# Keys of the dilated heads: the low part in both halves of a tile per head, and score matmuls of 128 rows

## The chip, the cores and the metric

The kernel runs on one core of a Trainium2 chip. The metric is the device time of one execution in microseconds (us), as the median of several runs.

## What is computed

Two layers of a decoder trunk on 512 tokens of width 1024, all in float32. Each layer is a hybrid token mixer, a cross attention into 256 memory tokens and a squared-ReLU MLP, with norms around each. The mixer has eight latent heads and eight dilated heads of 64 features; the change concerns the dilated ones alone:

```python
z = h @ w_in
q_d, k_d, v_d = z[..., o3:o4], z[..., o4:o5], z[..., o5:]
...
s = jnp.einsum('brcqhd,brckhd->brchqk', qq, kk, preferred_element_type=jnp.float32) * scale + bias
s = jnp.where(mask, s, -jnp.inf)
...
e = jnp.exp(s - s_max)
```

The three dilation patterns are merged by their softmax denominators. The kernel therefore computes one dense causal score matrix per head and adds a table by distance, which holds the bias and the logarithm of the number of patterns that reach a pair.

## The kernel before

**Split numbers.** Every float32 operand of a large matmul is kept as a high part and a low part (its remainder) of type fp32r, and a product is summed from several matmuls: in the linear layers (`mm`, lines 193 to 200) high by low, low by high and high by high. The names in the profile are `whi`, `wlo` for weights, `xth`, `xtl` for inputs.

**Dilated queries and keys.** `feat_major` (lines 618 and 619) leaves two heads in one tile of 128 features by 512 tokens in PSUM, head `a` on partitions 64`a` to 64`a`+63. `ev_qd` (line 571) makes one tile `qs` per head: its high part on the head's own 64 partitions and its low part on the other 64. `ev_kd` (line 582) makes one tile `kh` per head with the high part in both halves: ScalarE (ACT) writes the head's own half (line 588), GpSimd (POOL) copies it to the other (line 590). The low parts of two heads, written by VectorE (DVE, line 591), lie in one shared tile `kl`.

**Scores.** `dilated_parts` (line 594) gives the two matmuls of a score tile. The first has 128 rows (contraction over all partitions): (high q, low q) by (high k, high k). The second has 64 rows: high q by low k. `scores` (line 411) walks over four query tiles i of 128 queries; each has these two matmuls (line 419) of N = 128(i+1) columns into a PSUM tile `sp` (two buffers), then DVE adds the table and takes the minimum (line 423), ACT takes the exponential (line 425), DVE the reciprocal of the sum (line 426), and POOL scales the rows (line 427). TensorE (PE) then transposes the rows (`ptp`, lines 431 to 449) and multiplies by the values (`op`, line 456). The eight latent heads use the same function with three matmuls of 96 rows each (`latent_parts`, operands named `ring`).

**What sets the order.** `attention` (line 776) runs the scores one head ahead of the transposes, and `weave` (line 217) puts steps of other linear layers (`ptm`, `pfm`) between its steps by an estimate of PE's work. The tile scheduler then fixes each engine's order. Weights arrive on SyncE's (SP) one DMA queue as `raw`, in turn with the table `tb` of each dilated head (line 624). Most tiles, `qs`, `kh`, `kl` and `tb` among them, come from one pool of 49 buffers of 128x512 (`unit`, line 63).

Of the kernel before, what the change touches and what calls it, by code (L numbers as in the profile page):

```python
# [34 lines left out]
SPLIT = True  # L35
SCORE_STEPS = (0, 1, 2)  # query tiles after which the scores let other work in
FINE = 2  # weight pieces in one step of a linear layer
MEM_AT = 30  # step of the latent layers at which the memory is read
STOP = object()
DELAY = 7.5  # tensor engine work (us) put between a norm and its transposes  # L40
RATIOS = (1.8, 1.1)  # other work by attention work: dilated heads, latent heads


@with_exitstack
def block_kernel(ctx: ExitStack, tc, x, mem, positions, rel_bias, w_in, q_norm_g, w_uq, kv_norm_g,
# [3 lines left out]
    nc = tc.nc  # L49
# [24 lines left out]

# [1 line left out]
    ident = const.tile([128, 128], F32, name="ident")  # L76
# [11 lines left out]
    def load_x(t, src=None):  # L88
        """The residual stays on chip but for the mixer's attention, over which it is kept in memory."""
        for n in range(2):  # L90
            xs[t][n] = unit("xs")
            rows, cols = slice(t * 128, (t + 1) * 128), slice(n * 512, (n + 1) * 512)
            nc.sync.dma_start(xs[t][n], x[0, rows, cols] if src is None else src[rows, cols])
# [10 lines left out]
    def gains(c0, parts):  # L104
        """Gains as columns c0.. of gT, features on partitions."""
        grow = unit("grow", (80, 128))
        n = 0
        for g in parts:
            rows = g.shape[0] * g.shape[1] // 128
            nc.sync.dma_start(grow[n:n + rows, :], g.rearrange("l (n p) -> (l n) p", p=128))  # L110
            n += rows
        gps = t_ps("gps")
        nc.tensor.transpose(gps[:, 0:n], grow[0:n, :], ident[0:n, 0:n])
        nc.vector.tensor_copy(gT[:, c0:c0 + n], gps[:, 0:n])
# [4 lines left out]

# [1 line left out]
    def rpow(m, name):  # L121
# [4 lines left out]
    def rstd_from(ss, width, name):  # L126
        """(ss / width + eps) ** -0.5"""
        m = small(name + "m", ss.shape[1])
        nc.vector.tensor_scalar(m, ss, 1.0 / width, EPS, op0=OP.mult, op1=OP.add)
        return rpow(m, name)  # L130

    def load_w(src, r0, kts, c0, width, gcol=None, heads=0):
        """Rows r0.. (kts tiles of 128), columns c0..c0+width, as parts for the tensor engine;
        heads: columns [head, 2, 64] are reordered to [2, head, 64]."""
        raw = wp.tile([128, 2, 512], F32, tag="raw", name="raw", bufs=3)
# [31 lines left out]

    # Order of emission: `clk` adds up the tensor engine's work so far; work that waits for a chain
    # on the other engines is put off until that much of it has been emitted.
    clk = [0.0]  # L170
# [46 lines left out]
    def weave(main, fills, ratio):  # L217
        """Emit main, and after each of its steps about ratio() times its work from fills, the first
        that is not held up; a step that is held up yields True."""
        owed = 0.0  # L220
# [22 lines left out]
    def with_at(gen, other, at):  # L243
        """gen, with a step of other after each of its steps from step `at` on."""
        i = 0
        for held in gen:
            yield held
            i += not held
            if i > at and not held:
                next(other, None)  # L250
        run(other)

    def tok_major_steps(src, c0, width, nk, gcol, xh, xl, tiles, evac, r0=0, whole=False, rot=0, early=()):
        """out[token, column] = sum_k X[k, token] W[k, column]; evac(t, psum).
        whole: one token tile after the other, all weights of the group resident."""
        ps = [None] * tiles
# [34 lines left out]
    def feat_major_steps(src, c0, ntile, nk, gcol, xh, xl, ntok, evac, whole=0):  # L291
        """out[column, token]; ntile column tiles of 128; evac(m, psum).
        whole: in that many parts of the tokens, all weights of the group resident."""
        ps = [None] * ntile
# [43 lines left out]
    def transposed(xn, n, dests, t):  # L338
        """Half n of a token tile, transposed into columns t of dests."""
        tp = t_ps("tp")  # L340
# [30 lines left out]
    def add_post_norm(ys, ms, t):  # L371
        """xs[t] += y * g * rstd(y); ys = y * g in two halves, ms = their parts of the mean square."""
        m = small("pnm", 1)
# [12 lines left out]
    def out_proj_steps(w, OTh, OTl, gb, after, rot=0):  # L386
        """token-major projection of the eight feature tiles, then post-norm into the residual."""
        ys = [[None, None] for _ in range(NT)]
# [22 lines left out]
    def scores(P, parts, tb, scale):  # L411
        """Causal softmax of one head: rows of queries, tile i at OFFS[i]."""
        nm = small("nm", 4)
# [17 lines left out]
    def transposed_scores(P, pts):  # L431
        """The softmax with keys on partitions: key tile j holds queries from tile j on."""
        PT = pp.tile([128, 1280], F32, tag="PT", name="PT", bufs=2)
# [17 lines left out]
    def weighted_values(PTs, v_of):  # L451
        """Two heads' outputs, features on partitions, as one feature tile."""
        op = mm_ps("op")
# [12 lines left out]
    def rotary_tables():  # L466
        # angles reduced by multiples of two pi in exact steps
        posi = unit("posi", (4, 128), I32)
# [29 lines left out]
    def distance_tables():  # L498
        # relative-position table by distance: bias + log(number of patterns that reach the pair)
        rb = const.tile([32, HEADS], F32, name="rb")  # L500
# [11 lines left out]

# [1 line left out]
    for l in range(DEPTH):  # L514
        # mixer input
        if l == 0:
# [25 lines left out]
        def rope(dst, src, t, n):  # L542
            """dst[:, n, 32] = rotated src[:, n, 32] (may be the same)."""
            cosb = cs[:, t, 0:1, :].to_broadcast([128, n, ROPE])
# [26 lines left out]
        def ev_qd(m, ps):  # L571
            """Head a at partitions 64a: its high part there, its low part in the other half."""
            for a in range(2):
# [8 lines left out]
        def ev_kd(m, ps):  # L582
            """The high part of each head in both halves; the low parts of the two heads in one tile."""
            lo = unit("kl", dt=WD) if SPLIT else None
            for a in range(2):
                here, there = slice(a * 64, a * 64 + 64), slice(64 - a * 64, 128 - a * 64)
                u = unit("kh", dt=WD)
                nc.scalar.activation(u[here, :], ps[here, :], AF.Copy)
                if SPLIT:
                    nc.gpsimd.tensor_scalar(u[there, :], u[here, :].bitcast(F32), 1.0, 1.0, op0=OP.mult, op1=OP.mult)  # L590
                    nc.vector.tensor_sub(lo[here, :], ps[here, :], u[here, :].bitcast(F32))
                kd.append((u, lo))

        def dilated_parts(h):
            here = slice(h % 2 * 64, h % 2 * 64 + 64)
            if not SPLIT:
                return [(qd[h][here, :], kd[h][0][here, :])]
            return [(qd[h], kd[h][0]), (qd[h][here, :], kd[h][1][here, :])]

# [32 lines left out]
        def latent():  # L632
            """Queries, keys (features on partitions) and values of the latent attention."""
            yield from tok_major_steps(wl, QL, KVL + ROPE, NK, gm, xh_t, xl_t, NT, ev_ckv, whole=True)
# [86 lines left out]
        def slot(h):  # L721
            """Parts of a head's queries and keys, in turn over four places."""
            r, c = ring[h % 4 // 2], h % 2 * 4
            return (r[:, c, :], r[:, c + 1, :]), (r[:, c + 2, :], r[:, c + 3, :])
# [20 lines left out]
        def memory():  # L745
            """Keys (features on partitions) and values of the memory."""
            mt = [(unit("mth", (128, 2, MEM), WD), unit("mtl", (128, 2, MEM), WD) if SPLIT else None)
# [28 lines left out]
        def attention():  # L776
            """Dilated heads, then latent heads; the scores run one head ahead."""
            P, PTs = [None] * 16, [None] * 16
# [33 lines left out]

        # cross attention
        qx = []
# [42 lines left out]
        def cross_transposed(h, P):  # L857
            """Keys on partitions, in parts: [key tile][part]."""
            PT = []
# [70 lines left out]

        # MLP
        gb = row_bcast(post_mlp_g, l)
# [48 lines left out]
def _shape_constants():  # L981
    """Index tables of the shapes: entry j stands for the distance 511 - j between query and key."""
    d = 511 - np.arange(640)
# [26 lines left out]
```

## Time and profile before

| | |
|---|---|
| median of 3 runs | 1589.37 us (1587.48 to 1592.85) |
| profiled execution, span from first to last instruction | 1589.2 us |
| PE busy / weight loads (PEld) | 1559.9 us (98%) / 1299.1 us (82%) |
| DVE / ACT / POOL busy | 820.2 (52%) / 706.8 (44%) / 229.5 us (14%) |
| mean granted TensorE clock | 0.995 of full speed |

The page gives busy time of each engine, the chain of work that ended last, and the costliest groups. The profile shows no other time of the profiled execution than its span. A matmul's recorded time is longer than its share of a stream, because matmuls overlap: what one costs is read from the distance between the starts of consecutive ones in the timeline. In its rows "128*128" stands for active rows by active columns of the array, and "128x384" for what streams through it.

### The profile page before, as it was taken

The page shows a single profiled execution, that of the slowest core. Times are in us where ns is not written, and L with a number is a line of the kernel's source. Part 1 is how long each engine was busy: PE and PEld are TensorE (multiplying, and loading weights), DVE is VectorE, ACT ScalarE, POOL GpSimd, SP SyncE. Part 2 cuts the span into 40 slices and gives each one's busy share as a digit, 9 for nine tenths or more (in the row PEclk, how much of TensorE's full clock was granted, in tenths as well). Part 3 has the DMA queues.
Part 4 walks back from the last instruction along what each step waited for, and adds up shares of the span by engine and source line. Part 5 has one row for each costly group of instructions (what it writes and reads, how often), then busy time and mean ns, then how long its engine had stood idle before and what let it go on. Part 6 is the DMA issues. An engine that isn't in the chain of part 4 may idle for free.

```text
span 1589.2 us, 21074 instructions
## 1 busy us (share of the span) xinstructions
PE 1559.9 (98%) x8023; PEld 1299.1 (82%) x8023; DVE 820.2 (52%) x1567; ACT 706.8 (44%) x1414; POOL 229.5 (14%) x417
## 2 busy tenths in 40 slices
PE   7999999999999999999999999999999999999998
PEld 5787788898898888888878877978988988888886
DVE  4554775456464344433564567654555544434344
ACT  4454666355353242423344566654454433333241
POOL 2023631022020000000021255201111000000000
PEclk9998999999999999999999999999999999999999
DMA  5432223513124323233342222253221432332321
GB/s 159 160 89 82 72 69 110 189 57 116 53 68 132 106 93 93 96 103 93 93 132 61 95 81 77 68 167 126 93 80 51 133 95 93 99 100 93 96 90 53
DMA packets 82793, 155.68 MB, mean 98 GB/s; under 512 B 5718, under 2 KB 11524, under 8 KB 82692
## 3 DMA queue, kind: packets, MB, share of 16 engines
q1 hardware_dynamic: 82692, 154.33, 30.9%
q8 instruction: 63, 1.03, 0.3%
q14 instruction: 38, 0.31, 0.1%
HBM read 150.10 MB, written 6.84 MB: 99 GB/s over the span
## 4 chain that ended last, share of the span: by engine, by line
PE 90%; DVE 4%; issue 2%; POOL 2%; ACT 1%; DMA 1%; SPq 0%; POOLq 0%; DVEq 0%; ACTq 0%
PE ptm L198 14%; PE ptm L199 13%; PE ptm L200 13%; PE pfm L199 12%; PE pfm L198 12%; PE pfm L200 12%; PE sp L419 4%; PE op L190 2%; PE ptp L186 2%; DVE wlo L160 2%; PE tp L186 1%; PE opx L198 0%; PE opx L200 0%; PE opx L199 0%; POOL xn L362 0%
## 5 line engine op out<-in xcount | busy, mean ns | idle before, releaser
L155 ACT ACTIVATE whi<-raw,gT 128x512 fp32r<-128x512 f32 (+2 forms) x324 | 210.0, 697 | 264.4 <-PE ptm L200 125.8
L160 DVE SCALAR_TENSOR_TENSOR wlo<-raw,gT,whi 128x512 fp32r<-128x512 f32 (+3 forms) x332 | 230.1, 728 | 186.7 <-ACT whi L155 185.0
L199 PE MATMUL pfm<-xth,wlo 128*128 128x512 f32 (+1 forms) x896 | 322.7, 360 | 0.5
L198 PE MATMUL pfm<-xtl,whi 128*128 128x512 f32 (+1 forms) x896 | 322.4, 360 | 0.0
L200 PE MATMUL pfm<-xth,whi 128*128 128x512 f32 (+1 forms) x896 | 321.7, 359 | 0.0
L151 DVE TENSOR_TENSOR wlo<-raw,whi 128x1024 fp32r<-128x1024 f32 x96 | 117.5, 1224 | 214.8 <-ACT whi L150 211.9
L150 ACT ACTIVATE whi<-raw 128x1024 fp32r<-128x1024 f32 x96 | 101.7, 1060 | 223.3 <-PE ptm L200 117.2
L198 PE MATMUL ptm<-wlo,hh 128*128 128x512 f32 x512 | 199.5, 390 | 0.0
L200 PE MATMUL ptm<-whi,hh 128*128 128x512 f32 x512 | 199.3, 389 | 0.0
L199 PE MATMUL ptm<-whi,hl 128*128 128x512 f32 x512 | 199.3, 389 | 0.0
L199 PEld LDWEIGHTS pfm<-xth,wlo 128*128 128x128 f32 x896 | 169.2, 189 | 26.5 <-DVE wlo L160 1.4
L198 PEld LDWEIGHTS pfm<-xtl,whi 128*128 128x128 f32 x896 | 169.2, 189 | 25.4 <-ACT whi L155 0.5
L200 PEld LDWEIGHTS pfm<-xth,whi 128*128 128x128 f32 x896 | 169.2, 189 | 25.3 <-issue 0.5
L123 POOL TENSOR_TENSOR pnr<-pnm,mhalf 128x1 f32<-128x1 f32 x24 | 15.8, 659 | 859.4 <-DVE pnm L374 859.3
L199 PEld LDWEIGHTS ptm<-whi,hl 128*128 128x128 f32 x512 | 96.1, 188 | 20.0
L198 PEld LDWEIGHTS ptm<-wlo,hh 128*128 128x128 f32 x512 | 96.1, 188 | 19.9
L200 PEld LDWEIGHTS ptm<-whi,hh 128*128 128x128 f32 x512 | 96.1, 188 | 19.8
L427 POOL TENSOR_SCALAR P<-P,rs 128x128 f32<-128x128 f32 (+3 forms) x128 | 71.7, 564 | 155.3 <-DVE rs L426 91.9
L425 ACT ACTIVATE P<-P,nm 128x128 f32<-128x128 f32 (+3 forms) x128 | 71.1, 557 | 26.5 <-DVE nm L423 25.4
L198 PE MATMUL ptm<-wlo,xth 128*128 128x512 f32 (+2 forms) x192 | 69.2, 360 | 1.7 <-ACT xth L164 1.7
L199 PE MATMUL ptm<-whi,xtl 128*128 128x512 f32 (+2 forms) x192 | 67.1, 350 | 0.4 <-DVE xtl L166 0.4
L200 PE MATMUL ptm<-whi,xth 128*128 128x512 f32 (+2 forms) x192 | 66.1, 344 | 0.0
(212 smaller groups left out, 2604.3 us busy)
## 6 DMA issues: line engine op xcount, KB each, us to landing
raw<-in_w_up SPq DMA_DIRECT2D x64, 512.0 KB, 3.7
raw<-in_w_down SPq DMA_DIRECT2D x64, 512.0 KB, 3.4
raw<-in_w_in SPq DMA_DIRECT2D x24, 512.0 KB, 3.8
raw<-in_w_xk SPq DMA_DIRECT2D x16, 512.0 KB, 3.4
raw<-in_w_xv SPq DMA_DIRECT2D x16, 512.0 KB, 3.9
raw<-in_w_mix_out SPq DMA_DIRECT2D x16, 512.0 KB, 4.8
raw<-in_w_xq SPq DMA_DIRECT2D x16, 512.0 KB, 3.4
raw<-in_w_xo SPq DMA_DIRECT2D x16, 512.0 KB, 4.4
```

The source lines that it names most:

```text
L150: nc.scalar.activation(hi[:, :kts, :width], raw[:, :kts, :width], AF.Copy)
L151: nc.vector.tensor_sub(lo[:, :kts, :width], raw[:, :kts, :width], hi[:, :kts, :width].bitcast(F32))
L155: nc.scalar.activation(cols(hi, k, False), cols(raw, k, True), AF.Copy, scale=g)
L160: nc.vector.scalar_tensor_tensor(lv, rv, g, hv, op0=OP.mult, op1=OP.subtract)
L186: nc.tensor.transpose(out_, in_, ident_)
L190: nc.tensor.matmul(ps, lhsT=lhsT, rhs=rhs, start=start, stop=stop)
L198: nc.tensor.matmul(ps, lhsT=lh, rhs=rl, start=first, stop=False)
L199: nc.tensor.matmul(ps, lhsT=ll, rhs=rh, start=False, stop=False)
L200: nc.tensor.matmul(ps, lhsT=lh, rhs=rh, start=False, stop=last)
L419: nc.tensor.matmul(sp[:, :L], lhsT=q[:, i * 128:(i + 1) * 128], rhs=k[:, :L], start=n == 0, stop=n == len(parts) - 1)
L425: nc.scalar.activation(Pi, Pi, AF.Exp, bias=nm[:, i:i + 1], scale=-1.0, accum_out=rs[:, i:i + 1])
L427: nc.gpsimd.tensor_scalar(Pi, Pi, rs[:, i:i + 1], 1.0, op0=OP.mult, op1=OP.mult)
```

## The change

Each head gets a low tile of its own. DVE writes the head's half as before, and POOL copies it to the other half, as it does with the high part. The second score matmul then takes the whole `qs` tile and the whole low tile: 128 rows, (high q, low q) by (low k, low k), which adds the product of the two low parts. The rest of the difference are comments.

```diff
         def ev_kd(m, ps):
-            lo = unit("kl", dt=WD) if SPLIT else None
             for a in range(2):
                 here, there = slice(a * 64, a * 64 + 64), slice(64 - a * 64, 128 - a * 64)
                 u = unit("kh", dt=WD)
                 nc.scalar.activation(u[here, :], ps[here, :], AF.Copy)
+                lo = None
                 if SPLIT:
-                    nc.gpsimd.tensor_scalar(u[there, :], u[here, :].bitcast(F32), 1.0, 1.0, op0=OP.mult, op1=OP.mult)
+                    lo = unit("kl", dt=WD)
                     nc.vector.tensor_sub(lo[here, :], ps[here, :], u[here, :].bitcast(F32))
+                    for w in (u, lo):
+                        nc.gpsimd.tensor_scalar(w[there, :], w[here, :].bitcast(F32), 1.0, 1.0, op0=OP.mult,
+                                                op1=OP.mult)
                 kd.append((u, lo))
...
-            return [(qd[h], kd[h][0]), (qd[h][here, :], kd[h][1][here, :])]
+            return [(qd[h], kd[h][0]), (qd[h], kd[h][1])]
```

On POOL, in the first layer, between the last norm and the first softmax, where the keys' copies stand (`kh` and `kl` are the high and low key tiles). Before:

```order
L362 TENSOR_SCALAR xn_216<-xs_203,n1r_212 128x512 [waits DMAHW2_49]
L590 TENSOR_SCALAR kh_660<-kh_660 64x512 [waits Activation_49,Pool_49]
L590 TENSOR_SCALAR kh_664<-kh_664 64x512 [waits PE_49,Activation_49]
L590 TENSOR_SCALAR kh_694<-kh_694 64x512 [waits Activation_49]
L590 TENSOR_SCALAR kh_698<-kh_698 64x512 [waits PE_49,Activation_49]
```

And now:

```order
L362 TENSOR_SCALAR xn_216<-xs_203,n1r_212 128x512 [waits DMAHW2_49]
L593 TENSOR_SCALAR kh_659<-kh_659 64x512 [waits Activation_49,Pool_49]
L593 TENSOR_SCALAR kl_661<-kl_661 64x512 [waits DVE_49]
L593 TENSOR_SCALAR kh_665<-kh_665 64x512 [waits PE_49,Activation_49]
L593 TENSOR_SCALAR kl_667<-kl_667 64x512 [waits DVE_49]
L593 TENSOR_SCALAR kh_696<-kh_696 64x512 [waits Activation_49]
L593 TENSOR_SCALAR kl_698<-kl_698 64x512 [waits DVE_49]
```

Behind each copy of a high part stands one of a low part, which waits for DVE; eight more per layer, sixteen in all.

On PE, in the first layer, at the first score tile of the first dilated head (`pfm` is the key projection, `ptm` the next linear layer):

```order
 L200 MATMUL pfm<-xth,whi 128x512
 L419 MATMUL sp<-kh,qs 128x128 [waits Pool_49]
-L419 MATMUL sp<-kl,qs 128x128 [waits DVE_49]
+L419 MATMUL sp<-kl,qs 128x128 [waits Pool_49]
 L198 MATMUL ptm<-wlo,xth 128x288 [waits DVE_49,PE_49]
```

The second matmul waits for POOL's copy where it waited for DVE's subtraction; in this layer nothing on PE changes its place.

On PE, in the second layer, at the first dilated head's larger score tiles (`ptp` are the transposes of the softmax):

```order
+L199 MATMUL ptm<-whi,xtl 128x288
+L200 MATMUL ptm<-whi,xth 128x288
+L198 MATMUL ptm<-wlo,xth 128x288
 L419 MATMUL sp<-kh,qs 128x384
 L419 MATMUL sp<-kl,qs 128x384
-L199 MATMUL ptm<-whi,xtl 128x288
 L419 MATMUL sp<-kh,qs 128x512
 L419 MATMUL sp<-kl,qs 128x512
+L199 MATMUL ptm<-whi,xtl 128x288
 L200 MATMUL ptm<-whi,xth 128x288
-L198 MATMUL ptm<-wlo,xth 128x288
+L186 MATMUL ptp<-ident,P 128x128
```

A few matmuls of the linear layer and a transpose change places with the score tiles. The second layer has four such pieces of difference, and the number of matmuls stays.

## Rows read from the trace of the kernel before

**Rows 1.** The page: busy time, and the chain that ended last by engine.

```profile
PE 1559.9 (98%) x8023; PEld 1299.1 (82%) x8023; DVE 820.2 (52%) x1567; ACT 706.8 (44%) x1414; POOL 229.5 (14%) x417
...
PE 90%; DVE 4%; issue 2%; POOL 2%; ACT 1%; DMA 1%; SPq 0%; POOLq 0%; DVEq 0%; ACTq 0%
```

**Rows 2.** Instructions of line 419: duration min/median/max ns, first and last start us.

```profile
L419 PE MATMUL sp<-kl,qs x64: 322/435/792, 87.3 to 955.1; 64*128 64x128 f32 x16, 64*128 64x256 f32 x16, 64*128 64x384 f32 x16, 64*128 64x512 f32 x16
```

**Rows 3.** Timeline, PE, first layer: start us, us, engine, line, op, out<-in.

```profile
88.27 0.29 PE L200 MATMUL ptm<-whi,xth 128*128 128x288 f32 x1
88.40 0.28 PE L419 MATMUL sp<-kh,qs 128*128 128x256 f32 x1
88.61 0.39 PE L419 MATMUL sp<-kl,qs 64*128 64x256 f32 x1
88.93 0.40 PE L198 MATMUL ptm<-wlo,xth 128*128 128x288 f32 x1
89.17 0.29 PE L199 MATMUL ptm<-whi,xtl 128*128 128x288 f32 x1
89.29 0.30 PE L200 MATMUL ptm<-whi,xth 128*128 128x288 f32 x1
```

**Rows 4.** Timeline, PE, second layer, tiles of 128 and 256 columns.

```profile
910.05 0.22 PE L419 MATMUL sp<-kh,qs 128*128 128x128 f32 x1
910.20 0.33 PE L419 MATMUL sp<-kl,qs 64*128 64x128 f32 x1
910.45 0.39 PE L419 MATMUL sp<-kh,qs 128*128 128x256 f32 x1
...
911.36 0.34 PE L199 MATMUL ptm<-whi,xtl 128*128 128x384 f32 x1
```

**Rows 5.** Timeline, PE, first layer: first and last of tiles of 384 and 512 columns.

```profile
92.19 0.34 PE L419 MATMUL sp<-kh,qs 128*128 128x384 f32 x1
...
93.91 0.29 PE L199 MATMUL ptm<-whi,xtl 128*128 128x288 f32 x1
```

**Rows 6.** Timeline, PE: three matmuls of a latent head, and the transposes behind.

```profile
242.63 0.86 PE L419 MATMUL sp<-ring 96*128 96x512 f32 x3
243.33 0.93 PE L186 MATMUL ptp<-ident,P 128*128 128x128 f32 x7
244.01 0.36 PE L198 MATMUL pfm<-mtl,whi 128*128 128x256 f32 x1
```

**Rows 7.** Timeline, weight loads (PEld), first layer.

```profile
86.65 0.19 PEld L200 LDWEIGHTS pfm<-xth,whi 128*128 128x128 f32 x1
86.88 0.19 PEld L419 LDWEIGHTS sp<-kh,qs 128*128 128x128 f32 x1
87.25 0.18 PEld L419 LDWEIGHTS sp<-kl,qs 64*128 64x128 f32 x1 [0.18 <-issue]
```

**Rows 8.** Instructions on the tile kh, and POOL's timeline, first layer.

```profile
L590 POOL TENSOR_SCALAR kh<-kh x16: 612/614/617, 71.7 to 875.3; 64x512 fp32r<-64x512 f32 x16
...
89.45 0.62 POOL L590 TENSOR_SCALAR kh<-kh 64x512 fp32r<-64x512 f32 x1 [0.80 <-ACT kh L588]
93.74 0.37 POOL L427 TENSOR_SCALAR P<-P,rs 128x128 f32<-128x128 f32 x1 [3.68 <-DVE rs L426]
```

**Rows 9.** Chain that ended last (start us, us, what), and a wait of 86 to 176 us.

```profile
96.81 0.99 POOL P L427
...
925.78 3.93 DMA tb<-tabw
...
PEld ptp L186 <- POOL P L427: 0.3, 1, 0.3
```

**Rows 10.** Busy time by stretch: us, PE PEld DVE ACT POOL, clock, DMA share, GB/s.

```profile
86.80:175.30 88.50, 86.53 (x462) 66.84 (x460) 52.81 (x161) 52.05 (x132) 33.88 (x73) 0.94 0.29 90
872.20:955.60 83.40, 81.81 (x461) 64.06 (x459) 50.71 (x157) 48.44 (x125) 33.28 (x73) 1.00 0.31 99
144.40:154.60 10.20, 9.98 (x27) 6.03 (x27) 5.06 (x18) 3.95 (x11) 3.15 (x5) 0.50 0.46 154
```

## The prediction

> **What bounds the kernel now.** I began with the page. PE is busy 98% of the span and makes up 90% of the chain that ended last [rows 1], so what is saved on PE is worth its full length until another wait ends later. A busy PE says nothing on how well it is fed, so I went on to PE's timeline and looked only at the distances between starts. In a stream of full-height matmuls this distance follows the columns: 0.12 to 0.13 us at 288 columns [rows 3], and three matmuls of 512 columns take 0.70 us, 0.233 each [rows 6]. That is some 0.45 ns per column, the ordinary price below.
>
> The dilated score tiles stand out against it. In the first layer a pair of 256 columns starts at 88.40; its 64-row matmul comes 0.21 us later, the next full-height matmul 0.32 after that, and the one behind is again late, 0.24 for 288 columns [rows 3]. From 88.40 to 89.17 are 0.77 us; the same 800 columns cost 0.36 at the ordinary price. So one pair with a single 64-row matmul in it costs about 0.4 us more than its columns. PEld shows where it goes: the load for a full-height matmul starts together with the matmul ahead of it, every 0.23 us without a gap, while that of the 64-row matmul starts only 0.37 us after the load ahead, with 0.18 us idle behind "issue", that is waiting for no other engine, and together with its own matmul [rows 7]. Each step from 128 rows to 64 and each step back lets PE run empty, and a pair has one of each.
>
> Is it the 64 rows, or the score tiles as such? The latent heads answer: their three matmuls of 96 rows of 512 columns stand between full-height ones and take 0.70 us, no more than the columns [rows 6]. So fewer than 128 rows cost nothing by themselves; a height of 64 does.
>
> **The change, part by part.** *The second matmul gets 128 rows.* There are 64 of them, 16 of each width [rows 2]; each has a 128-row partner, and a head gives two sets of two pairs.
> - Widths 128 and 256, second layer: from 910.05 to 911.36 are 1.31 us [rows 4]. At the ordinary price the pair of 256 and the 384 columns of the matmul behind cost 0.41. For a 128-column matmul I bound the price by its columns (0.06) and by the seven transposes of 128 columns, 0.10 each (0.68 us from their first start to the next matmul's, [rows 6]); nearer is the transpose, since it too loads 128 columns of weights for 128 streamed. Two at 0.10 make 0.61 in all, and the set saves 0.70; at the other end 0.78. I take 0.72.
> - Widths 384 and 512, first layer: from 92.19 to 93.91 are 1.72 us [rows 5] for 2080 columns, 0.94 at the ordinary price. The set saves 0.78.
>
> Sixteen heads in two layers, each with both sets: 16 x (0.72 + 0.78) = **24.0 us**. Where other work stands between the two pairs of a set the saving is the same, 0.4 per pair [rows 3].
>
> *The added copies.* POOL gets 16 more copies of 0.614 us [rows 8], 9.8 us on an engine that is busy 14% [rows 1]. What hides them: in the first layer the last copy of a high part starts at 89.45 and ends at 90.07; the one behind it ends some 0.6 later, near 90.7, and POOL's next work, the first softmax, starts only at 93.74 after 3.68 us idle, waiting for DVE [rows 8]. The first low copy is due at the second score matmul, 87.3 [rows 2], and the first high copy ran at 71.7 [rows 8], so the low one is done near 73. If the cover were gone, POOL's softmax of the first head would be late by one copy, 0.6 us per layer. Priced at 0. DVE does as many subtractions as before.
>
> *What cannot be passed on.* At the first head PE already waits for POOL's softmax: it is the only such wait of PEld in the first layer's stretch, 0.3 us, behind a POOL step of 0.99 us on the chain [rows 9]. What PE gains between that head's last score tile and its transposes only lengthens this wait: two pairs, 0.7 us, and I take the same for the second layer. There the chain also runs through a transfer of `tb` of 3.93 us from 925.78 on [rows 9]; the two pairs just ahead of it, 0.7 us, are lost too. Sum of losses 2.1 us. Everything else sits on PE: the stretch from the first to the last dilated head is 88.5 and 83.4 us long, of which PE is busy 86.5 and 81.8 [rows 10].
>
> *The moved matmuls* in the second layer are a few linear matmuls past score tiles; they issue the same work, and no transfer on SP changes its place. The bound is one wait of the first head, 0.3 us either way [rows 9]; priced at 0.
>
> **Sum:** 1589.2 - 24.0 + 2.1 = 1567.3 us. The profiled span lies 0.2 us under the median of the runs, so it needs no correction: **1567.5 us**.
>
> **The clock.** From 144.4 to 154.6 us the granted clock is 0.50, that is 1.2 in place of 2.4 GHz; the same stretch of the second layer has none, and the first layer's is 5.1 us longer [rows 10]. I read this as the price of one such drop. With the PE waits shifted, the drop may go or the second layer may get one. So 5 us belong to the range on either side, not to the forecast.
>
> **The rivals.**
> *Serial weight loads.* The gap in front of the 64-row matmul is a weight load that does not overlap [rows 7]; were that the fate of any load onto rows in use, a full-height one would wait alike, and nothing is saved: 1589. Against it stands the same view, where full-height loads overlap full-height matmuls without a gap [rows 7]. The Trainium skill, "TensorE: Matmul & The Clock Gate", Part 3, says that LDWEIGHTS overlaps running matmuls only when their row groups differ, which speaks against this change; the trace of this case does not agree for full-height neighbours. Chance 0.04.
>
> *The gain turns into waits.* The softmax chain over DVE, ACT, DVE and POOL does not get shorter, and PE reaches each transpose about 1.5 us per head sooner. For it: the wait that the first head has already. Against it: the other seven heads of the first layer show no wait for POOL at all [rows 9]. If half the pairs lost their gain, 12 us would be left: 1577. Chance 0.12.
>
> *Slower, by buffers.* Four more of the 49 shared buffers per layer are held until the last dilated score. A `tb` that finds no free buffer blocks the one queue, and the weights behind it. A late transfer costs up to 3.9 us [rows 9]; six of sixteen would eat the 24 us, and eight, 31 us, would give 1589 + 7 = 1596. Against it: SP's order is unchanged, and only one of sixteen lies on the chain now. Chance 0.03.
>
> *It does not do what it says:* if a step of height 96 to 128 is free only because those matmuls share their neighbours' form, a residual of 0.1 us per matmul could stay, 64 x 0.1 = 6 us: 1574. Chance 0.08, since 96-row matmuls next to full ones show none [rows 6].
>
> **How the numbers follow.** The forecast, 1562 to 1573 with either state of the clock, has 0.73. The range 1560 to 1577 takes in all 24 us with the clock drop gone (1589.2 - 24 - 5 = 1560), the residual and the half gain. About 0.3%, 5 us, is what a measurement of this kernel tells from no change. Serial loads are "same" with part of the unnamed rest, 0.05; buffers are "slower", 0.03; all else is faster, 0.92.
>
> **What would show it.** Right: `kl` matmuls read 128*128, their loads start with the matmul ahead, and a set of 384 and 512 columns takes 0.95 us to the second matmul behind instead of 1.72; POOL has 32 key copies of 0.61 us, and the dilated stretch is 10 to 11 us shorter in each layer at equal clock. Wrong: the same distances with 128 rows (serial loads), PEld idle before `ptp` for POOL at many heads (waits), SP idle before `tb` with PE idle behind it (buffers), or a second stretch at clock 0.5.

## The result, and the profile after

The changed kernel took 1575.86 us (median of 4 runs, 1574.59 to 1579.42), the kernel before 1588.46 us (4 runs, 1587.48 to 1592.85). The ratio is 0.9922, 95% interval 0.9902 to 0.9943: 12.6 us faster. The forecast was 1567.5, its range 1560 to 1577. The time lies in the range, but above the likeliest window (1562 to 1573), close to the 1577 of the rival in which half of the gain turns into waits.

The page after, busy time and chain by engine, answers to [rows 1]:

```profile
PE 1539.8 (98%) x8023; PEld 1295.8 (82%) x8023; DVE 819.8 (52%) x1567; ACT 706.7 (45%) x1414; POOL 241.2 (15%) x433
...
PE 86%; DVE 6%; issue 3%; DMA 2%; ACT 2%; POOL 1%; SPq 0%; DVEq 0%; POOLq 0%; ACTq 0%
```

PE is 20 us less busy, POOL has 16 instructions and 11.7 us more, and the number of matmuls is the same. But PE's share of the chain fell from 90% to 86%: DVE, DMA and ACT took most of what it lost. That is the short form of this case.

The instructions on the tile `kl`, after; they answer to [rows 2, 8]:

```profile
L419 PE MATMUL sp<-kl,qs x64: 274/310/628, 88.5 to 940.6; 128*128 128x128 f32 x16, 128*128 128x256 f32 x16, 128*128 128x384 f32 x16, 128*128 128x512 f32 x16
...
L593 POOL TENSOR_SCALAR kl<-kl x16: 612/615/1042, 73.7 to 867.7; 64x512 fp32r<-64x512 f32 x16
```

All 64 second matmuls now have 128 rows, and the added copies take 0.615 us each (median), as priced; the longest took 1.042. PE's timeline after, a set of 128 and 256 columns with linear matmuls of 384 behind it (compare [rows 4]), then a set of 384 and 512 columns in front of transposes:

```profile
899.55 0.22 PE L419 MATMUL sp<-kh,qs 128*128 128x128 f32 x1
899.61 0.27 PE L419 MATMUL sp<-kl,qs 128*128 128x128 f32 x1
899.72 0.33 PE L419 MATMUL sp<-kh,qs 128*128 128x256 f32 x1
899.89 0.28 PE L419 MATMUL sp<-kl,qs 128*128 128x256 f32 x1
900.00 0.34 PE L198 MATMUL ptm<-wlo,xth 128*128 128x384 f32 x1
900.18 0.33 PE L199 MATMUL ptm<-whi,xtl 128*128 128x384 f32 x1
...
903.03 0.33 PE L419 MATMUL sp<-kh,qs 128*128 128x384 f32 x1
903.20 0.34 PE L419 MATMUL sp<-kl,qs 128*128 128x384 f32 x1
903.37 0.40 PE L419 MATMUL sp<-kh,qs 128*128 128x512 f32 x1
903.61 0.39 PE L419 MATMUL sp<-kl,qs 128*128 128x512 f32 x1
903.84 0.49 PE L186 MATMUL ptp<-ident,P 128*128 128x128 f32 x3
```

The first set takes 0.63 us to the second matmul behind it, where it took 1.31 [rows 4]: 0.68 saved, 0.72 was forecast. The second takes 0.81 us to the transposes for 1792 columns, just the ordinary price of 0.45 ns per column. Weight loads (PEld) after, further on in the first layer, and the matmul that starts with the second of them; compare [rows 7]:

```profile
127.25 0.19 PEld L419 LDWEIGHTS sp<-kh,qs 128*128 128x128 f32 x1
127.43 0.19 PEld L419 LDWEIGHTS sp<-kl,qs 128*128 128x128 f32 x1
127.43 0.33 PE L419 MATMUL sp<-kh,qs 128*128 128x384 f32 x1
```

The load for `kl` starts with the matmul ahead of it (127.43) and without idle time; the wait for "issue" is gone: before, PEld sat so 9.7 us at the score tiles (next view), and the view of after has no such line. So the mechanism is there at its forecast price. The question is where 8 of some 20 us went. Two totals of the waits view show it, first before (not shown ahead of the prediction), then after (us in total, times, longest):

```profile
PEld sp L419 <- issue: 9.7, 44, 0.4
PEld sp L419 <- DVE nm L423: 5.4, 13, 1.0
...
DVE P L423 <- DMA tb<-tabw: 0.5, 1, 0.5
```

```profile
PEld sp L419 <- DVE nm L423: 12.0, 19, 2.2
...
DVE P L423 <- DMA tb<-tabw: 8.7, 6, 3.6
```

The score matmuls wait for DVE to empty one of the two `sp` buffers, and DVE waits for the table `tb`, six times in place of once. The stretch from the first to the last dilated head, with the edges of [rows 10], and the two places where the clock was at half (us, PE, PEld, DVE, ACT, POOL, clock, DMA share, GB/s):

```profile
88.10:166.84 78.74, 74.38 (x464) 64.08 (x463) 52.24 (x162) 51.86 (x132) 35.55 (x75) 0.98 0.32 100
863.44:941.04 77.60, 72.52 (x462) 62.54 (x461) 50.41 (x158) 48.02 (x125) 34.74 (x75) 1.00 0.32 103
...
29.00:32.40 3.40, 3.40 (x11) 2.82 (x12) 1.98 (x3) 1.13 (x2) 0.00 (x0) 0.50 0.02 5
141.60:145.00 3.40, 2.96 (x10) 2.27 (x10) 2.24 (x11) 2.47 (x7) 1.66 (x3) 0.50 0.83 292
```

The first layer's stretch is 9.8 us shorter, but 3.4 of that is a shorter stay at half clock (10.2 us before [rows 10], 3.4 now, at half a microsecond lost per microsecond); the second layer's, without a drop in either, is 5.8 us shorter. At equal clock that is 6 us per layer, not the 10 to 11 of the forecast.

### The profile page after: what moved, and what is told of

The parts are those of the page before. It is cut to its first block, busy times and chain, and to the rows that moved or that the text cites. A ratio compares the mean times of both kernels' runs of the same rounds, so it can differ in the third digit from the quotient of the medians.

```text
span 1574.8 us, 21092 instructions
## 1 busy us (share of the span) xinstructions
PE 1539.8 (98%) x8023; PEld 1295.8 (82%) x8023; DVE 819.8 (52%) x1567; ACT 706.7 (45%) x1414; POOL 241.2 (15%) x433
## 4 chain that ended last, share of the span: by engine, by line
PE 86%; DVE 6%; issue 3%; DMA 2%; ACT 2%; POOL 1%; SPq 0%; DVEq 0%; POOLq 0%; ACTq 0%
PE ptm L198 13%; PE ptm L199 13%; PE ptm L200 13%; PE pfm L199 12%; PE pfm L198 12%; PE pfm L200 12%; PE sp L419 3%; DVE wlo L160 3%; PE op L190 2%; PE ptp L186 2%; DMA tb<-tabw 1%; PE tp L186 1%; PE opx L198 1%; DVE P L423 0%; PE opx L200 0%
## 5 line engine op out<-in xcount | busy, mean ns | idle before, releaser
L199 PEld LDWEIGHTS ptm<-whi,hl 128*128 128x128 f32 x512 | 96.1, 188 | 19.8
```

The source lines that it names most:

```text
L199: nc.tensor.matmul(ps, lhsT=ll, rhs=rh, start=False, stop=False)
```

## The experiments

**The theories.** A: the gain is the height's alone, some 22 us on PE, of which 6 to 8 turn into waits, since PE now outruns the tables and weights on SP's queue. B: the height gives the full 22 us, and the added copies and tiles cost 6 to 9.

**How the runs are compared.** Runs of one kernel differ mainly by how long the clock was at half: the 15 runs of the kernel before beside the first four experiments go from 1585.1 to 1592.4 us at mean granted clocks from 0.999 to 0.995. A run's time less (1 - mean clock) x span is about what it would take at full clock, an estimate that holds as far as PE is the bound; by it the same 15 runs lie within 3.3 us. I give it as "at full clock", as a median, beside the measured time; the clock is on record to 0.001, so each value is rounded by up to 0.8 us. The experiments come from four chips, with the kernel before beside each: at full clock it took 1583.6 us beside the first four, then 1585.3, 1584.7 and, beside the last, 1585.1; the changed kernel took 1572.5. So a difference between two runs from different chips is uncertain by about 2 us.

### Is it the height?

**The height alone.** Before's shared low tile, no copies. The added rows then multiply a head's low queries by its neighbour's low keys; this holds for every run below that has more than 64 rows without the further tiles.

```diff
-            return [(qd[h], kd[h][0]), (qd[h][here, :], kd[h][1][here, :])]
+            return [(qd[h], kd[h][0]), (qd[h], kd[h][1])]
```

> The kernel before, with its shared low tile, but the second score matmul takes the whole tile: 128 rows, no added copy, no added buffer. The product then also holds low part of q by the other head's low part of k, a term of the size of the one that the change adds. The order on every engine stays that of the kernel before. Theory A (the gain is the height of the matmul alone, some 22 us on PE, of which 6 to 8 us turn into waits because PE now outruns the tables and weights that come over SP's queue): as the changed kernel, 12 to 15 us under the kernel before. Theory B (the full 22 us are gained, and the copies and buffers cost 6 to 9 us): 20 to 22 us under the kernel before.

Measured: 1573.96 us, before 1587.78; ratio 0.9919 (0.9905 to 0.9933), 13.8 us less; at full clock 1570.6, 13.0 less. The height alone gives all that the change gave, as A says; by B it had to give the full 22.

**All but the height.** The changed kernel with before's second matmul of 64 rows:

```diff
-            return [(qd[h], kd[h][0]), (qd[h], kd[h][1])]
+            return [(qd[h], kd[h][0]), (qd[h][here, :], kd[h][1][here, :])]
```

> The changed kernel with its low tile per head and all 16 added copies, but the second score matmul takes only the head's own 64 rows again. Theory A: as the kernel before, within 2 us. Theory B (copies and buffers cost): 6 to 9 us slower than the kernel before.

Measured: 1594.56 us, ratio 1.0048 (1.0034 to 1.0062); at full clock 1588.0, 4.4 over before. So the rest of the change costs time when the height is left out, which I had priced at nothing. A, too, expected less than 2 us; its size is nearer to B, and the next runs ask where it comes from.

**Does 96 rows switch too?**

```diff
-            return [(qd[h], kd[h][0]), (qd[h][here, :], kd[h][1][here, :])]
+            rows = slice(0, 128 if h % 2 else 96)
+            return [(qd[h], kd[h][0]), (qd[h][rows, :], kd[h][1][rows, :])]
```

> Edit: the height alone (shared low tile, no copies), but the second matmul of each even head has 96 rows and of each odd head 128. If only the step between 128 and 64 rows costs a switch, this is as the height alone, 1572 to 1576 us, and the pairs of even heads stand at the same distance as those of odd ones. If any step away from 128 rows costs one, half of the gain of 13.8 us goes, 1579 to 1583 us, and the pairs of even heads are some 0.4 us longer. A residual of 0.1 us per matmul of 96 rows would be 3 us: 1577.

Measured: 1574.94 us, ratio 0.9911 (0.9899 to 0.9923); at full clock 1571.1. As the height alone. PE's timeline of this run, a set of an even head:

```profile
897.81 0.22 PE L419 MATMUL sp<-kh,qs 128*128 128x128 f32 x1
897.87 0.28 PE L419 MATMUL sp<-kl,qs 96*128 96x128 f32 x1
897.98 0.33 PE L419 MATMUL sp<-kh,qs 128*128 128x256 f32 x1
898.15 0.28 PE L419 MATMUL sp<-kl,qs 96*128 96x256 f32 x1
898.27 0.34 PE L198 MATMUL ptm<-wlo,xth 128*128 128x384 f32 x1
898.45 0.34 PE L199 MATMUL ptm<-whi,xtl 128*128 128x384 f32 x1
```

0.64 us with 96 rows, 0.63 with 128, 1.31 with 64 [rows 4]. A step between 128 and 96 rows is free, one between 128 and 64 is not, as I had read from the latent heads [rows 6]. The Trainium skill, "TensorEngine Tiling (Array Packing)", Key Properties, says that a change of tiling mode drains TensorE, and its list of modes has 64 rows but not 96; the trace agrees. From the distances of all 64 pairs below, the switch there and back costs 0.36 us on average.

### What do the added tiles and copies cost?

**The tiles without the copies, 64 rows** (PE, DVE and SP issue in the changed kernel's order):

```diff
-            lo = unit("kl", dt=WD) if SPLIT else None
             for a in range(2):
...
+                    lo = unit("kl", dt=WD)
```

> Edit: the kernel before with a low tile per head, but no low copy, and the second matmul with 64 rows of it. PE, DVE and SP issue in the order of the changed kernel, POOL as before. If the 6.8 us that the copies, buffers and order cost at 64 rows (1594.56 us) come from the buffers and the order they bring, this is 1592 to 1595 us; if they come from the copies on POOL, it is 1587 to 1590, as the kernel before.

Measured: 1594.60 us, before 1590.12; ratio 1.0029 (1.0016 to 1.0041); at full clock 1587.7, 2.4 over before.

**The copies without the tiles:** the copy of each high part is made twice.

```diff
                     nc.gpsimd.tensor_scalar(u[there, :], u[here, :].bitcast(F32), 1.0, 1.0, op0=OP.mult, op1=OP.mult)
+                    nc.gpsimd.tensor_scalar(u[there, :], u[here, :].bitcast(F32), 1.0, 1.0, op0=OP.mult, op1=OP.mult)
```

> Edit: the kernel before with the copy of each high key part made twice on POOL, so that POOL has the 16 further copies of 0.61 us and nothing else changes: no further tile, order of PE and DVE as before, 64 rows. If the copies themselves cost the 6.8 us, 1592 to 1595 us; if the buffers and their order do, 1587 to 1590. In the first case the waits of PE stand at the first head, where DVE and POOL make the keys; in the second they stay as before.

Measured: 1590.07 us, ratio 1.0005 (0.9991 to 1.0018). In this order the copies cost nothing that the time shows, as forecast (the interval leaves room for up to 2.9 us); the tiles do. The copy made twice here waits for no DVE step, as the low copy of the change does, so that wait is not tried by this run.

How four more tiles per layer cost time can be followed link by link. In the second layer of the kernel before, DVE subtracts a `wlo` (which frees a `raw` buffer) ahead of the four scalings of `ckv`, which wait for POOL; the next weight and the tables follow on SP. DVE's and SP's timeline, before:

```profile
900.02 0.61 DVE L160 SCALAR_TENSOR_TENSOR wlo<-raw,gT,whi 128x384 fp32r<-128x384 f32 x1
901.55 1.14 DVE L639 TENSOR_SCALAR ckv<-ckv,rkvr 128x256 f32<-128x256 f32 x4 [0.92 <-POOL rkvr L123]
...
905.80 0.29 DVE L423 CUSTOM_DVE_ANT_0 P<-sp,tb 128x128 f32<-128x128 f32 x1 [2.65 <-PE ptp L186]
```

```profile
899.51 0.38 SPq L136 DMA_DIRECT2D raw<-in_w_ukv  x1
900.69 0.38 SPq L136 DMA_DIRECT2D raw<-in_w_uq  x1
901.18 0.88 SPq L624 DMA_DIRECT2D tb<-tabw  x2
```

With the further tiles the scheduler puts the `ckv` scalings ahead of that `wlo`. The chain that ended last of the changed kernel shows what follows (start us, us, what):

```profile
889.23 1.03 POOL rkvr L123
890.28 1.14 DVE ckv L642 x4
891.43 0.54 DVE wlo L160
891.98 0.38 SPq L136
892.41 3.47 DMA tb<-tabw
896.01 0.29 DVE P L423
896.37 0.62 PE sp L419 x2
```

POOL, `ckv`, `wlo`, the weight on SP, the table behind it, its transfer, DVE's first step of the head, PE. SP asks for this weight 3.7 us after the one ahead (888.24 to 891.98, from SP's timeline), before 1.2. PE starts its last matmul at 893.99 and gets its `sp` buffer only at 896.37. With 64 rows and the further tiles it is the same place: PE's timeline of the run without copies shows a wait of 2.5 us that the kernel before has not,

```profile
905.28 0.44 PE L419 MATMUL sp<-kh,qs 128*128 128x384 f32 x1 [2.46 <-DVE nm L423]
```

about the 2.4 us that this run lost at full clock. DVE waits 4.71 us for the table just ahead of it. Most of the rest of its 4.5 us by medians is clock: its runs have a mean granted clock of 0.9961, those of before beside it 0.9969, 1.3 us.

**The same with the tables early.** The tiles without copies, 64 rows, and each head's `tb` asked for two heads earlier:

```diff
+        tbs = [dil_table(h) for h in range(2)]
         feat_major(wl, o3 + 512, 4, NK, gm, xh_f, xl_f, S, ev_kd, whole=1)
...
+                    if i + 2 < 8:
+                        tbs.append(dil_table(i + 2))
-                    yield from scores(P[i], dilated_parts(i), dil_table(i), 1.0)
+                    yield from scores(P[i], dilated_parts(i), tbs[i], 1.0)
```

> Edit: the kernel with a low tile per head and 64 rows (1594.6 us), with each head's table asked for two heads earlier. Theory A: the further tiles cost time through one place, a table that comes late in the second layer (2.7 us) and the clock behind it. With the tables early the cost is gone, and this runs as the kernel before with early tables (1585.2 us): 1583 to 1588. If the buffers cost time in another way (weights that wait for a free tile), it stays 3 us or more above that: 1589 to 1594.

Measured: 1583.97 us, before 1589.84; ratio 0.9963 (0.9948 to 0.9978); at full clock 1582.3. The further tiles cost nothing any more (the same tables in the kernel before, below, give 0.9976). But the edit did more than to ask early: in this run DVE has the `wlo` ahead of the `ckv` scalings again, as in the kernel before. DVE's timeline of this run:

```profile
894.46 0.61 DVE L160 SCALAR_TENSOR_TENSOR wlo<-raw,gT,whi 128x384 fp32r<-128x384 f32 x1
895.99 1.14 DVE L644 TENSOR_SCALAR ckv<-ckv,rkvr 128x256 f32<-128x256 f32 x4 [0.92 <-POOL rkvr L123]
```

So it is shown that the tiles by themselves cost nothing, and that the cost lies in the order that they brought. That it passes through the late table rests on the chain above and the 2.46 us; the order and the early table were not tried apart.

### Where the rest of the gain went

**Early tables, in the changed kernel and in the kernel before** (the diff above in each):

> The changed kernel with the table tb of each dilated head asked for two heads earlier (the first two ahead of the key projection); up to two more buffers are held for it. Theory A: DVE's waits for tb (8.7 us, six times) go; of the PE waits behind them some 4 to 5 us come back: 16 to 18 us under the kernel before. Theory B (copies and buffers): as the changed kernel, or slower by the two buffers more.

> The kernel before with the same earlier tables. DVE waited for tb once there, 0.5 us. Theory A: as the kernel before, at most 1.5 us faster. If the tables were late in themselves, and not because PE came sooner: faster by the same 4 to 5 us.

Measured: 1573.15 us with the change, ratio 0.9913 (0.9900 to 0.9927); 1585.20 without it, ratio 0.9976 (0.9967 to 0.9986). At full clock 1570.3 and 1583.6. The kernel before gains nothing at full clock; its 2.6 us are clock. DVE no longer waits for a table in either. But with the change only some 2 us came back (14.6 us under the kernel before, where 16 to 18 were expected), not the 4.4 that the waits for tables had taken (5.2 us against 0.8 before, below): other waits took their place. PE's and POOL's timelines in the first layer, and PE's in the second, with the change:

```profile
98.12 0.44 PE L186 MATMUL ptp<-ident,P 128*128 128x128 f32 x2 [1.86 <-POOL P L427]
...
95.41 1.17 POOL L593 TENSOR_SCALAR kl<-kl 64x512 fp32r<-64x512 f32 x1
...
97.37 0.69 POOL L427 TENSOR_SCALAR P<-P,rs 128x512 f32<-128x512 f32 x1
...
913.20 0.38 PE L419 MATMUL sp<-kh,qs 128*128 128x256 f32 x1 [0.51 <-DVE nm L423]
916.53 0.62 PE L198 MATMUL ptm<-wlo,ch 128*128 128x384 f32 x2 [0.69 <-ACT ch L164]
```

The longest, 1.86 us, is for POOL at the first head: with the tables early the scheduler puts key copies between POOL's softmax steps of that head, and from 94.83 to 97.27 POOL makes three of them, a low one of 1.17 us among them, while the reciprocal that the next softmax step needs was ready at 94.75. In this order, then, the copies are not free; without the low copies (next run) PE waits 0.38 us for POOL there.

**The height with early tables,** without further tiles (the two diffs together):

> Edit: before's shared low tile, second matmul over all 128 rows (so that it adds low query by the neighbour head's low key), no copies, no further buffers, and each head's table asked for two heads earlier. If the part of the gain that was lost went mainly into waits for the tables, this should end below the height alone (1573.96 us) by 2 to 4 us, 1570 to 1572. If other waits at the score tiles take the tables' place, as they did with the changed kernel (1573.15 us), it ends at 1572 to 1575. Theory B (copies and buffers cost 6 to 9 us) would want 1564 to 1567, since none of them is here.

Measured: 1570.52 us, before 1590.12; ratio 0.9879 (0.9866 to 0.9892), 19.6 us less; at full clock 1568.2. 2.1 us faster at full clock than the changed kernel with early tables, of which 1.6 us are PE's longer waits for POOL there (2.0 us in all against 0.4); the order differs too, so the two were not tried apart. But it is 17.1 us under the kernel before at full clock, still 5 short of 22, with no copies and no further tiles to blame: B, as it was put, is out.

**More linear work between the dilated heads,** on top of that; `RATIOS[0]` sets how much linear work is put after each step of the dilated heads.

```diff
-RATIOS = (1.8, 1.1)
+RATIOS = (2.1, 1.1)
```

> Edit: the height with early tables (1570.52 us), and the number that sets how much linear work is put between the dilated heads raised from 1.8 to 2.1. Theory A: about 5 us of the 22 are still lost there, because PE reaches score tiles and transposes before DVE, ACT and POOL are done; with more linear matmuls between them most of these waits go, 1565 to 1568 us, unless the linear work runs out before the last dilated head, which then waits as much: 1569 to 1572. If the waits do not come from too little work in between, 1569 to 1573.

The same with 1.95:

> Edit: as the run before it, with 1.95 in place of 1.8. Half as much further linear work between the heads: by theory A half of the waits go, 1567 to 1569 us; otherwise 1569 to 1573.

Measured: with 2.1 1574.99 us, ratio 0.9908 (0.9888 to 0.9928); with 1.95 1564.76 us, ratio 0.984 (0.9818 to 0.9862), 25.1 us less than before and the fastest kernel of this study. Neither time was expected: the first lies above 1573, the second below 1567. With 2.1 the linear work runs out early, and PE waits in the first latent heads; its timeline there:

```profile
175.43 0.63 PE L186 MATMUL tp<-ident,mr 128*128 128x128 f32 x4 [1.40 <-DVE rs L426]
176.99 0.39 PE L198 MATMUL pfm<-mtl,whi 128*128 128x256 f32 x1 [0.93 <-DVE mtl L166]
```

With 1.95 these are absent, and PEld's wait for DVE at the score tiles is half of that with 1.8 (waits view of the two, 1.8 first):

```profile
PEld sp L419 <- DVE nm L423: 11.5, 28, 1.0
```

```profile
PEld sp L419 <- DVE nm L423: 6.0, 18, 0.9
```

I took that as proof that the number gives back what the height had lost, and ran the control: early tables and 1.95 in the kernel before.

> Edit: the control of the run with 1.95 (1564.76 us): early tables and 1.95 in the kernel before, 64 rows as there. Theory A: the waits that 1.95 takes away are mostly there because the height switches are gone, so the number brings little here: 1582 to 1586 us beside 1585.2 with 1.8, and the height is worth 18 to 21 us between these two. If the number is worth 6 us whatever the height, 1578 to 1581 us, and the height is worth 13 to 16 as in the kernel before.

Measured: 1579.93 us, before 1587.14; ratio 0.9953 (0.9937 to 0.9970). The number is worth 5.3 us without the height too (5.8 with it), so my reading was wrong: 1.95 is a better schedule for either kernel. The height is worth 15.2 us between these two by medians; but they come from different chips, and against the kernel before beside each it is 17.9 us by medians and 14.1 at full clock. That it is worth more here than elsewhere is not shown.

### The account

The height alone, by medians and at full clock; and from the traces, summed over the 64 dilated pairs and the matmul behind each, what the distances exceed the ordinary price by (0.227 us for 512 columns, 0.174 for 384, 0.132 for 288, 0.120 for 256, 0.108 for 128), with single waits of over 0.25 us, up to the second latent head, apart (all us, both layers). In the first two rows all engines of the two kernels issue in the same order; in the last two they do not (PE has nine pieces of difference, DVE ten or more, and a table on SP changes its place), and the two kernels come from different chips:

| order | 64 rows | 128 rows | difference | at full clock | excess of pairs | waits over 0.25 |
|---|---|---|---|---|---|---|
| before | 1587.8 | 1574.0 | -13.8 | -13.0 | 23.1 to 4.0 | |
| further tiles and copies | 1594.6 | 1575.9 | -18.7 | -15.5 | | |
| early tables | 1585.2 | 1570.5 | -14.7 | -15.4 | 23.3 to 2.7 | 6.6 to 11.7 |
| early tables, 1.95 | 1579.9 | 1564.8 | -15.2 | -14.5 | 23.0 to 2.5 | 5.1 to 8.8 |

The excess of pairs falls by some 20 us in each (the 4.0 holds over 1 us of matmuls at half clock), and 4 to 5 of it come back as waits where the tables are early: 20.6 less 5.1 is 15.5 in the third row, measured 15.4, or 17.1 against the kernel before beside each; in the fourth 16.8 stand against 14.5 or 14.1. From before to the changed kernel it falls from 23.1 to 3.3, 19.8 us; the waits of over 0.25 us up to the last dilated head rise from 2.5 to 6.6 us in the first layer (the stretch at half clock left out) and from 2.1 to 6.3 in the second, 8.3 us. That leaves 11.5, with 11.1 to 12.8 measured at full clock, by which group of runs of the kernel before is taken. The account closes within some 2 us; the limit of 0.25 us is my choice.

What most of the 8.3 us are: five waits behind a table at the third score tile of a head, 5.2 us in all, with 0.8 at such tiles before; five of 0.3 to 0.6 at the first head of the first layer and one in the second, 2.1 us, where the next keys, `wlo` and the first softmax are made; and 0.66 at the last head of each layer behind DVE.

## Why the prediction was right, and where it was off

- **The mechanism** (time is lost at each step between 128 and 64 rows, none between 128 and 96) is shown: by the loads, by the height alone, and by 96 rows.
- **24.0 us on PE.** 23.1 us of excess were there by all pairs, 19.8 went. What stays, 3.3 us, is 0.05 per pair, largely at a first matmul behind a transpose or a wait: the residual that a rival had put at 6 us, for another reason.
- **What cannot be passed on: 2.1 us.** This is the step that failed; it measured 8.3. I looked for the waits that before already showed, one at POOL and one transfer of `tb`, and wrote that only one of sixteen tables lies on the chain. In the changed kernel five do, for 20.2 us (4.57, 4.16, 4.46, 3.47 and 3.52). In before the waits view showed 0.5 us, for one. I had read a wait of zero as a margin, and it was not even zero: the table asked for at 901.18 took 4.5 us to land, and DVE's step at 905.80, shown above, starts 0.13 us after that, the same 0.13 us as behind the table of 892.41 in the changed kernel. The view puts the 2.65 us that DVE sat idle there down to PE's transposes alone. That the empty time at each switch had been a cover as well, in which DVE emptied the two `sp` buffers, fits the rows; no run tries it alone.
- **The moved matmuls, priced at 0, no transfer on SP moved.** SP's order indeed did not change, but DVE's did, and SP's weights wait for DVE. Two engines' order was not enough. At 64 rows this cost 2.4 us, and clock; with 128 rows 1.9 us or less, between the height alone and the changed kernel, since PE waits for the same table with the height alone (DVE waits 8.9 us for tables there, 8.7 in the changed kernel).
- **The copies, priced at 0:** right for the order that the change has, 1.0005. That POOL's order could put them ahead of the first head's softmax, as it does with the tables early, was bounded at 0.6 us per layer; there PE waited 1.86 us.
- **The clock:** the range for it was needed. The stay of 10.2 us at half clock became two of 3.4, which costs 3.4 us in place of 5.1.
- **The rivals.** Serial loads: excluded by the rows above; the sentence of the Trainium skill, "TensorE: Matmul & The Clock Gate", Part 3, that a load overlaps only where row groups differ does not hold for these full-height loads (127.43 above). Gain turns into waits: a third of it did (8.3 of 24), so the time came near to that case, but at the score tiles, behind DVE and its tables, not behind POOL at the transposes. Buffers: the mechanism (a table and weights behind it late) was real and had been given 0.03, as an event that turns the sign; it was a part of the ordinary case.
- **The sum** was made against the span. In the runs the time is the span and 1.8 us, so 1567.5 should have read 1569.1.

## What to carry to other kernels

A matmul of 64 rows among full ones costs a switch there and one back, together 0.36 us here on average; fill the other half if anything harmless can stand there. Before booking such a gain, ask for each transfer and each step of another engine that feeds the stretch by how much it comes early, for one that comes just in time shows little or no wait, or a wait under another name, and takes the gain when the consumer is faster. And compare the order of all engines: a tile more in a full pool can move one instruction on an engine that PE never waits for, and through it a queue.

## What the runs showed of the hardware that I had not expected

The mean granted clock differs between runs of one kernel, 0.992 to 0.999 for the kernel before, and explains most of their scatter (the 15 runs above). It is also a part of what an edit is worth: the kernel before loses 3.6 to 5.2 us on average by (1 - clock) x span, with early tables 1.9, with the further tiles at 64 rows 6.2. In the profiles the drops ahead of the kernel's end stand within some 1.5 us of PE's longer waits (in before, 2.0 us of waits between 142.1 and 144.6 us stand at the start of the drop of [rows 10]). A wait alone does not bring one: the 2.46 us at 905.28 without copies, and 2.0 us in the second layer of the changed kernel, stand without a drop. What decides stays open.

Where a POOL key copy and DVE's `wlo` subtraction, which reads `raw` and `whi`, run side by side, one of them or both are slower. In the changed kernel three of the 16 low copies ran beside a `wlo` and took 0.94, 0.87 and 1.04 us in place of 0.61; the three `wlo` beside the first took 1.73 us in place of 1.38 before (at 90.12). With the copies made twice the one at 89.58 kept its 0.62 us and the three `wlo` took 1.81. The copies beside DVE's `kl` subtraction kept their 0.61 us. POOL's and DVE's timelines after:

```profile
91.49 0.94 POOL L593 TENSOR_SCALAR kl<-kl 64x512 fp32r<-64x512 f32 x1
...
91.44 1.73 DVE L160 SCALAR_TENSOR_TENSOR wlo<-raw,gT,whi 128x288 fp32r<-128x288 f32 x3
```

It cost nothing that the time shows: the run with the copies made twice has three such meetings and takes as long as the kernel before.

What stays open: why the copies and tiles together (1.0048) seem to cost 2 us more than the tiles alone (1.0029), which the intervals do not exclude to be chance; how much of the 1.86 us behind POOL is the copies' and how much the order's; and whether more than two `sp` buffers would give back the last 4 us, which was not tried.
